# A decoder layer on one core: PE's instructions in the order in which the program writes them, sums of weight blocks one half product earlier

## The chip, the core and the metric

The kernel runs on one core of one Trainium2 chip. A core has five engines with a queue of instructions each: PE (TensorE, matmuls), DVE (VectorE), ACT (ScalarE), POOL (GpSimd) and SP (SyncE, which here only issues DMAs). They meet in semaphores: an instruction waits until those that it depends on have signalled. The metric is the time of one execution on the device, in microseconds (us), as the median of several runs.

## What is computed

One layer with three gated branches over 256 positions of width 2048 in float32, cut to what matters:

```python
q_a, k_a, v_a, z_a, u_g, v_g, z_g, q_c, z_c, g_logit = split(x @ w_in)   # 9 of width 1024, g_logit 6144
y_a = block_attention(q_a, k_a, v_a) * silu(z_a)              # 8 heads, causal
y_g = spatial_gating(u_g, v_g, w_s, ...) * silu(z_g)          # 8 groups
y_c = memory_attention(q_c, mem @ w_mem_k, mem @ w_mem_v) * silu(z_c)    # 4 heads
gates = sigmoid(g_logit)                                      # one per branch
merged = gates[0] * (y_a @ w_branch_attn) + gates[1] * (y_g @ w_branch_sgu) + gates[2] * (y_c @ w_branch_mem)
out = layer_norm(alpha * x + merged @ w_out)
```

With 256 positions there is one block of the block attention, so each head is causal attention over 256 keys.

## The kernel before

**Products.** Every large product of float32 values is made of three passes: each operand is split into a high and a low part (hi and lo), and hi x hi, hi x lo and lo x hi are added up in PSUM. `split(hi, lo, v)` is two instructions: ACT copies v to hi (L59), DVE subtracts hi from v (L60). A weight therefore passes DMA, ACT and DVE before PE can use it.

**Two streams.** The *classic* stream (a generator, `classic()`) multiplies weights half chunk by half chunk. Half chunk h17_0 is the first half of chunk 17, its parts are hi17_0 and lo17_0, 128x1024 each; there are three buffers for each part, and `c_half` prepares two halves ahead. Its parts in order: the gate of the memory branch (zc), queries (qc) and the memory attention, three tiles of za, a gated branch b2, the rest of za, queries and keys (q, k) of the block attention, three tiles of ug, branch b0, the rest of ug, zg with the spatial gating, branch b1. A *channel tile* (`channel_tile`, L187 and L188) is two halves of 8 k-steps, each with one 512-column and one 256-column matmul; a half of a branch (L712 to L714) is 12 matmuls of 512 columns.

The *S stream* (`s_stream`) makes the other projections with a fast matrix product: 8 units of 7 products (M1, M5, M6, M3, M7, M4, M2), each in two halves, 112 *half products* s0 to s111 of 12 matmuls (L386 to L388). Its weights are four blocks of a unit, B11, B12, B22 and B21 (in the listings b0 to b3), 128x2048 for each half. Before M5, M6 and M4 the block B11 is replaced by a difference (another block less B11) on DVE (L311); that is what "sum of weight blocks" means here. The block that a half product needs is then split into sh and sl (`s_prep`). These share a tag, shl, with four buffers, which is two half products: the split for half product s+2 can begin only when PE is done with half product s.

**Stages before the streams.** First the memory's values (mv) and keys (mk0 to mk7, channel tiles), then the two streams in turn. The driver takes 160 classic steps and, in proportion, 112 S steps, with a lead of 2 and a tail of 14 classic steps.

**Heads.** Each attention head has three small steps on PE: scores, transposes of the softmax's p (mpt0 to mpt3 for the memory heads, pt0 to pt7 for the others) and values. They are put in `pending`, and `tick` emits one step at the end of each classic tile. Between scores and transposes stand the maximum (DVE), two exponentials (ACT), a reciprocal and two scales (DVE, L587 for a block head: `p<-p,sm`).

**Order.** The lists `late` and `pending` set the order in which the program writes its instructions (the order of emission). The order in which an engine issues them is not that: for every engine a scheduler, which goes by a simulated timeline, chooses among the instructions whose operands it thinks ready. So on PE matmuls of the two streams are mixed finely, and a head's transposes come when the scheduler finds a place.

The names that the steps below touch: `s_prep` (splits and sums for a half product), `s_stream` (calls `s_prep(s + 2)` after half product s), `joined` (evacuates a channel tile: ACT copies one half of PSUM, named mk5l, zc0l and so on, DVE adds the other), `mem_head` and `moba_head` (the heads).

Of the kernel before, what the change touches and what calls it, by code (L numbers as in the profile page):

```python
# [11 lines left out]
ALU = mybir.AluOpType  # L12
# [15 lines left out]
def decoder_layer(ctx, tc, xT, memT, x_tok, w_st, w_mv, w_mk, w_zc, w_qc, w_za, w_qk, w_ug, w_zg,  # L28
                  w_br, w_o, w_sT, sgu_bc, ln_g, ln_b, out):
    nc = tc.nc  # L30

    const = ctx.enter_context(tc.tile_pool(name="const", bufs=1))
    big = ctx.enter_context(tc.tile_pool(name="big", bufs=1))
# [17 lines left out]
    def new_sps(name):  # L51
        return psum.tile([P, 512], F32, tag="sps", name=name, bufs=3)
# [5 lines left out]
    def split(hi, lo, v):  # L58
        nc.scalar.activation(hi, v, AF.Copy)  # L59
        nc.vector.tensor_tensor(lo, v, hi.bitcast(F32), op=ALU.subtract)  # L60
# [224 lines left out]
    UNITS = 8  # L285
    PRODUCTS = ("M1", "M5", "M6", "M3", "M7", "M4", "M2")
    FORM = {"M5": 1, "M6": 2, "M3": 4, "M7": 3}
    rt, shl, xsf, sp = {}, {}, {}, {}

    def s_load(u, blk, h):  # L290
        if u >= UNITS:
            return
        tag, bufs = ("rA", 2) if blk == 0 else ("rB", 4)
        t = wts.tile([P, 2048], F32, tag=tag, name=f"b{blk}_{u}_{h}", bufs=bufs)
        nc.sync.dma_start(t, w_st[u, blk, h])
        rt[u, blk, h] = t

    B11, B12, B22, B21 = range(4)

    def s_prep(s):  # L300
        u, r = divmod(s, 14)
        if u >= UNITS:
            return
        p, h = divmod(r, 2)
        p = PRODUCTS[p]
        if p in FORM:
            t = wts.tile([P, 4, 2 * P], F32R, tag="xsf", name=f"xf{s}", bufs=3)
            nc.sync.dma_start(t.bitcast(F32), xf_d[FORM[p], h])
            xsf[s] = t
        b = lambda blk: rt[u, blk, h]  # L310
        sub = lambda o, x, y: nc.vector.tensor_tensor(o, x, y, op=ALU.subtract)  # L311
        src = {"M1": B11, "M5": B11, "M6": B11, "M4": B11, "M3": B22, "M7": B12, "M2": B21}[p]
        if p == "M5":
            sub(b(B11), b(B12), b(B11))
        elif p == "M6":
            sub(b(B11), b(B22), b(B11))
        elif p == "M4":
            sub(b(B11), b(B21), b(B11))
        hi = wts.tile([P, 2048], F32R, tag="shl", name=f"sh{s}", bufs=4)
        lo = wts.tile([P, 2048], F32R, tag="shl", name=f"sl{s}", bufs=4)  # L320
        split(hi, lo, b(src))
        shl[s] = (hi, lo)
        if p == "M3":
            sub(b(B12), b(B22), b(B12))
            s_load(u, B21, h)
        elif p == "M7":
            s_load(u + 1, B12, h)
        elif p == "M4":
            s_load(u + 1, B11, h)
        elif p == "M2":  # L330
            s_load(u + 1, B22, h)

    def snap(name):
        return work.tile([P, 512], F32, tag="snap", name=name, bufs=5)

    def s_stream(finish):

        bank, kept = {}, {}

        def keep(name, ps):  # L340
            kept[name] = snap(name)
            nc.scalar.activation(kept[name], ps, AF.Copy)

        def result(u, t, n, ps, name):
            r = kept[name]
            nc.vector.tensor_tensor(r, ps, r, op=ALU.add)
            finish(u, t, n, r)

        def evacuate(u, p):
            if p == "M1":  # L350
                keep(f"k1_{u}", bank["b"])
            elif p == "M5":
                keep(f"k5_{u}", bank["d"])
            elif p == "M6":
                keep(f"k6_{u}", bank["b"])
            elif p == "M3":
                result(u, 0, 1, bank["d"], f"k6_{u}")
            elif p == "M7":
                keep(f"k7_{u}", bank["b"])
                result(u, 1, 1, bank["b"], f"k5_{u}")  # L360
            elif p == "M4":
                result(u, 1, 0, bank["c"], f"k7_{u}")
            else:
                result(u, 0, 0, bank["a"], f"k1_{u}")

        BANK = {"M1": "b", "M6": "b", "M7": "b", "M5": "d", "M3": "d", "M4": "c", "M2": "a"}
        for s in range(14 * UNITS):
            u, r = divmod(s, 14)
            p, h = divmod(r, 2)
            p = PRODUCTS[p]  # L370
            if h == 0 and p in ("M1", "M5", "M4", "M2"):
                bank[BANK[p]] = new_sps(f"s{p}_{u}")
            ps = bank[BANK[p]]
            hi, lo = shl.pop(s)
            for kk in range(4):
                k = 4 * h + kk
                if p in FORM:
                    ah, al = xsf[s][:, kk, 0:P], xsf[s][:, kk, P:2 * P]
                else:
                    k += 0 if p == "M1" else 8  # L380
                    t = P if p == "M4" else 0
                    ah, al = xhl[:, k, t:t + P], xhl[:, k, S + t:S + t + P]
                c = slice(kk * 512, (kk + 1) * 512)
                first = h == 0 and kk == 0 and p in ("M1", "M5", "M4", "M2")
                last = h == 1 and kk == 3
                nc.tensor.matmul(ps, ah, hi[:, c], start=first, stop=False, skip_group_check=True)  # L386
                nc.tensor.matmul(ps, ah, lo[:, c], start=False, stop=False, skip_group_check=True)  # L387
                nc.tensor.matmul(ps, al, hi[:, c], start=False, stop=last, skip_group_check=True)  # L388
            xsf.pop(s, None)
            s_prep(s + 2)  # L390
            if h == 1:
                late.append(lambda u=u, p=p: evacuate(u, p))
            yield
# [76 lines left out]
    while x_work:  # L470
        x_work.pop(0)()
        step(lambda: None)
    s_prep(0)
    s_prep(1)


    yhl = {}
# [297 lines left out]
    C_STEPS, S_STEPS = 160, 14 * UNITS  # L775
    LEAD, TAIL = 2, 14
    cs, ss = classic(), s_stream(s_finish)
    done_c = done_s = 0
    for _ in run(cs):
# [136 lines left out]
```

## Time and profile before

| | us |
|---|---|
| median of 3 runs | 1010.97 (1009.83 to 1012.68) |
| profiled execution, its own time | 1014.38 |
| its span | 1012.7 |
| PE busy | 982.4 (97%) |
| weight loads on PE, beside matmuls | 826.9 (82%) |
| DVE busy | 820.6 (81%) |
| ACT busy | 590.6 (58%) |
| POOL busy | 12.0 (1%) |
| mean granted TensorE clock | 0.99 |

The profiled execution lies above the median, so the numbers of a trace are set against its own time. A share of busy time is a mean over stages. PE's idle time stands where an instruction waits at the head of its queue, and the list of waits says for whom. Matmuls overlap: one of 512 columns is shown 0.39 us long, and the next starts 0.23 us after it. The granted clock of a stretch is 1.0 at 2.4 GHz and 0.5 at 1.2 GHz.

### The profile page before, as it was taken

How to read it: one execution, taken by the hardware profiler on the slowest of the kernel's cores; microseconds unless marked ns; L12 is line 12 of the kernel's file. 1: busy time of each engine (PE TensorE's matmuls, PEld its weight loads, DVE VectorE, ACT ScalarE, POOL GpSimd, SP SyncE). 2: the span in 40 equal slices, each digit the busy share in tenths (PEclk: the TensorE clock that was granted, in tenths of full speed). 3: DMA queues.
4: the chain of work that ended last, by engine and by line, in shares of the span. 5: the costliest groups of instructions: out<-in, count | busy, mean ns of one | idle time of the engine just before them, and what ended most of it. 6: DMA issues, size and time to landing. Idle time of an engine off the chain costs nothing.

```text
span 1012.7 us, 12913 instructions
## 1 busy us (share of the span) xinstructions
PE 982.4 (97%) x4888; PEld 826.9 (82%) x4888; DVE 820.6 (81%) x800; ACT 590.6 (58%) x646; POOL 12.0 (1%) x17
## 2 busy tenths in 40 slices
PE   9999899999999999999999999979998999999995
PEld 7788788888888788888888888858877888878885
DVE  5865987898779799888979898899979877676657
ACT  5654665565577566556556566867555559554430
POOL 0000000000000000000000000000000010000000
PEclk9999999999999999999999999989999999999998
DMA  8899589738965897598379648937994785778622
GB/s 330 313 387 414 181 304 348 277 132 296 364 223 168 295 382 278 165 362 346 134 271 356 236 139 281 382 106 269 414 366 147 284 286 183 249 259 303 238 84 83
DMA packets 68126, 269.28 MB, mean 266 GB/s; under 512 B 7521, under 2 KB 21601, under 8 KB 45537
## 3 DMA queue, kind: packets, MB, share of 16 engines
q1 hardware_dynamic: 68064, 268.47, 72.2%
q8 instruction: 38, 0.62, 0.2%
q14 instruction: 24, 0.19, 0.0%
HBM read 245.37 MB, written 23.07 MB: 265 GB/s over the span
## 4 chain that ended last, share of the span: by engine, by line
PE 85%; DVE 5%; ACT 4%; DMA 3%; issue 2%; POOL 0%; SPq 0%; DVEq 0%; ACTq 0%
PE sM L386 9%; PE sM L387 9%; PE sM L388 9%; PE b L713 4%; PE b L714 3%; PE b L712 3%; PE zc L187 3%; PE k L187 3%; PE qc L187 3%; PE za L187 3%; PE q L187 3%; PE mk L187 3%; PE o L800 3%; PE o L799 3%; PE o L798 3%; PE mv L423 3%
## 5 line engine op out<-in xcount | busy, mean ns | idle before, releaser
L59 ACT ACTIVATE hi<-raw 128x1024 fp32r<-128x1024 f32 (+1 forms) x218 | 228.3, 1051 | 191.4 <-PE o L800 29.1
L60 DVE TENSOR_TENSOR lo<-raw,hi 128x1024 fp32r<-128x1024 f32 (+1 forms) x218 | 263.1, 1214 | 77.2 <-ACT hi L59 76.4
L60 DVE TENSOR_TENSOR sl<-b,sh 128x2048 fp32r<-128x2048 f32 x112 | 256.3, 2291 | 57.1 <-ACT sh L59 56.7
L59 ACT ACTIVATE sh<-b 128x2048 fp32r<-128x2048 f32 x112 | 214.4, 1915 | 99.6 <-PE sM L387 89.3
L311 DVE TENSOR_TENSOR b<-b,b 128x2048 f32<-128x2048 f32 x64 | 146.3, 2289 | 8.0 <-DMA b<-in_w_st_dram 7.8
L386 PE MATMUL sM<-sh,xf 128*128 128x512 f32 x256 | 101.3, 396 | 6.5 <-ACT sh L59 6.5
L387 PE MATMUL sM<-sl,xf 128*128 128x512 f32 x256 | 100.6, 393 | 2.5 <-DVE sl L60 2.5
L388 PE MATMUL sM<-sh,xf 128*128 128x512 f32 x256 | 100.2, 391 | 0.0
L387 PE MATMUL sM<-sl,xhl 128*128 128x512 f32 x192 | 76.8, 400 | 0.6 <-DVE sl L60 0.6
L386 PE MATMUL sM<-sh,xhl 128*128 128x512 f32 x192 | 77.4, 403 | 0.0
L713 PE MATMUL b<-lo,yhl 128*128 128x512 f32 x192 | 76.1, 397 | 1.2 <-DVE lo L60 1.2
L388 PE MATMUL sM<-sh,xhl 128*128 128x512 f32 x192 | 76.3, 397 | 0.0
L714 PE MATMUL b<-hi,yhl 128*128 128x512 f32 x192 | 74.9, 394 | 0.0
L712 PE MATMUL b<-hi,yhl 128*128 128x512 f32 x192 | 74.0, 398 | 0.9 <-ACT hi L59 0.9
L386 PEld LDWEIGHTS sM<-sh,xf 128*128 128x128 f32 x256 | 48.3, 189 | 18.3 <-ACT sh L59 7.9
L387 PEld LDWEIGHTS sM<-sl,xf 128*128 128x128 f32 x256 | 48.2, 188 | 12.9 <-DVE sl L60 3.2
L388 PEld LDWEIGHTS sM<-sh,xf 128*128 128x128 f32 x256 | 48.1, 188 | 10.3
L187 PE MATMUL ug<-xhl,hi 128*128 128x512 f32 x128 | 46.3, 400 | 1.5 <-ACT hi L59 1.5
L187 PE MATMUL q<-xhl,hi 128*128 128x512 f32 x128 | 46.5, 399 | 0.0
L187 PE MATMUL qc<-xhl,hi 128*128 128x512 f32 x128 | 46.2, 400 | 0.0
L187 PE MATMUL zc<-xhl,hi 128*128 128x512 f32 x128 | 45.7, 398 | 0.4 <-ACT hi L59 0.4
L187 PE MATMUL k<-xhl,hi 128*128 128x512 f32 x128 | 46.0, 397 | 0.0
(296 smaller groups left out, 1853.1 us busy)
## 6 DMA issues: line engine op xcount, KB each, us to landing
b<-in_w_st_dram SPq DMA_DIRECT2D x64, 1024.0 KB, 7.2
xf<-xf SPq DMA_DIRECT2D x64, 512.0 KB, 6.0
raw<-in_w_br_dram SPq DMA_DIRECT2D x24, 1024.0 KB, 6.8
raw<-in_w_qk_dram SPq DMA_DIRECT2D x16, 1024.0 KB, 7.3
raw<-in_w_o_dram SPq DMA_DIRECT2D x16, 1024.0 KB, 5.4
raw<-in_w_mk_dram SPq DMA_DIRECT2D x8, 1024.0 KB, 10.1
raw<-in_w_zc_dram SPq DMA_DIRECT2D x8, 1024.0 KB, 6.5
raw<-in_w_qc_dram SPq DMA_DIRECT2D x8, 1024.0 KB, 7.6
```

The source lines that it names most:

```text
L59: nc.scalar.activation(hi, v, AF.Copy)
L60: nc.vector.tensor_tensor(lo, v, hi.bitcast(F32), op=ALU.subtract)
L187: nc.tensor.matmul(ps, hi, x, start=first, stop=False)
L311: sub = lambda o, x, y: nc.vector.tensor_tensor(o, x, y, op=ALU.subtract)
L386: nc.tensor.matmul(ps, ah, hi[:, c], start=first, stop=False, skip_group_check=True)
L387: nc.tensor.matmul(ps, ah, lo[:, c], start=False, stop=False, skip_group_check=True)
L388: nc.tensor.matmul(ps, al, hi[:, c], start=False, stop=last, skip_group_check=True)
L423: nc.tensor.matmul(ps[t][n], lhs, rhs[:, n * 512:(n + 1) * 512], start=(k == 0 and rhs is hi and lhs is xh[t]), stop=(k == KT - 1 and lhs ...
L712: nc.tensor.matmul(ps[t], yh, hi[:, c], start=(k == 0), stop=False)
L713: nc.tensor.matmul(ps[t], yh, lo[:, c], start=False, stop=False)
L714: nc.tensor.matmul(ps[t], yl, hi[:, c], start=False, stop=(k == 7))
L798: nc.tensor.matmul(ps[:, 0:n], mh, hi, start=first, stop=False)
```

## The change

PE is taken from the scheduler: its instructions stand in the order of emission. The other four engines are still ordered by the scheduler. And the subtraction that turns B11 into the block for M5, M6 or M4 leaves `s_prep` for a function of its own, `s_sum`, which is called for half product s+3 after half product s, ahead of `s_prep(s + 2)`, and for half product 2 ahead of the streams. The other subtraction, of B12 in M3's preparation, stays.

```diff
--- before.py
+++ after.py
@@ -28,6 +28,7 @@
 def decoder_layer(ctx, tc, xT, memT, x_tok, w_st, w_mv, w_mk, w_zc, w_qc, w_za, w_qk, w_ug, w_zg,
                   w_br, w_o, w_sT, sgu_bc, ln_g, ln_b, out):
     nc = tc.nc
+    ctx.enter_context(tc.manual_schedule(engines={mybir.EngineType.PE}))
 
     const = ctx.enter_context(tc.tile_pool(name="const", bufs=1))
     big = ctx.enter_context(tc.tile_pool(name="big", bufs=1))
@@ -297,6 +298,17 @@
 
     B11, B12, B22, B21 = range(4)
 
+    def s_sum(s):
+
+        u, r = divmod(s, 14)
+        if u >= UNITS:
+            return
+        p, h = divmod(r, 2)
+        other = {"M5": B12, "M6": B22, "M4": B21}.get(PRODUCTS[p])
+        if other is not None:
+            o = rt[u, B11, h]
+            nc.vector.tensor_tensor(o, rt[u, other, h], o, op=ALU.subtract)
+
     def s_prep(s):
         u, r = divmod(s, 14)
         if u >= UNITS:
@@ -310,12 +322,6 @@
         b = lambda blk: rt[u, blk, h]
         sub = lambda o, x, y: nc.vector.tensor_tensor(o, x, y, op=ALU.subtract)
         src = {"M1": B11, "M5": B11, "M6": B11, "M4": B11, "M3": B22, "M7": B12, "M2": B21}[p]
-        if p == "M5":
-            sub(b(B11), b(B12), b(B11))
-        elif p == "M6":
-            sub(b(B11), b(B22), b(B11))
-        elif p == "M4":
-            sub(b(B11), b(B21), b(B11))
         hi = wts.tile([P, 2048], F32R, tag="shl", name=f"sh{s}", bufs=4)
         lo = wts.tile([P, 2048], F32R, tag="shl", name=f"sl{s}", bufs=4)
         split(hi, lo, b(src))
@@ -387,6 +393,7 @@
                 nc.tensor.matmul(ps, ah, lo[:, c], start=False, stop=False, skip_group_check=True)
                 nc.tensor.matmul(ps, al, hi[:, c], start=False, stop=last, skip_group_check=True)
             xsf.pop(s, None)
+            s_sum(s + 3)
             s_prep(s + 2)
             if h == 1:
                 late.append(lambda u=u, p=p: evacuate(u, p))
@@ -472,6 +479,7 @@
         step(lambda: None)
     s_prep(0)
     s_prep(1)
+    s_sum(2)
 
 
     yhl = {}
```

All engines issue the same instructions as before, but for the loads of ACT's function table, of which there are 34 in place of 30. Three places show what moves. In the listings a row is a line of the program, the operation, output and inputs; a number at the end of a name is a buffer's.

PE around the transposes of head 1 of the block attention (pt1; q4 and q3 are the channel tiles of two later heads' queries), before:

```order
L188 MATMUL q4_4352<-xhl_96,lo56_0_4277 128x256
L187 MATMUL q4_4352<-xhl_96,hi56_0_4276 128x512
L597 MATMUL pt1_4155<-ident_83,p1_4074 128x128
L188 MATMUL q4_4352<-xhl_96,lo56_0_4277 128x256
L597 MATMUL pt1_4155<-ident_83,p1_4074 128x128 x2
L187 MATMUL q4_4352<-xhl_96,hi56_0_4276 128x512
```

and after, where the last matmuls of half product s57 stand ahead (sM1_4 is its PSUM tile):

```order
L392 MATMUL sM1_4_4094<-sh57_4017,xhl_98 128x512
L393 MATMUL sM1_4_4094<-sl57_4018,xhl_98 128x512
L394 MATMUL sM1_4_4094<-sh57_4017,xhl_98 128x512
L605 MATMUL pt1_4158<-ident_85,p1_4077 128x128 x3
L188 MATMUL q3_4166<-xhl_98,hi54_0_4045 128x512
L189 MATMUL q3_4166<-xhl_98,lo54_0_4046 128x256
```

In the order of emission all three transposes stand between s57 and the first half of q3; before, they stood within q4, two tiles later.

DVE at the same head (p1 is its softmax, sm1 its sum; sl58 to sl60 are low parts of S half products, lo55 and lo56 of classic halves, kT2 and qT3 other heads' evacuations), before:

```order
L60 TENSOR_TENSOR sl59_4149<-b0_4_1_3795,sh59_4148 128x2048
L311 TENSOR_TENSOR b0_4_0_3753<-b2_4_0_3843,b0_4_0_3753 128x2048
L60 TENSOR_TENSOR lo55_1_4207<-raw55_4022,hi55_1_4206 128x1024
L585 RECIPROCAL sm1_4077<-sm1_4077 128x2
L60 TENSOR_TENSOR lo56_0_4277<-raw56_4115,hi56_0_4276 128x1024
L208 TENSOR_TENSOR qT3_4161<-q3_4163,q3l_4247 128x256
L311 TENSOR_TENSOR b0_4_1_3795<-b2_4_1_3927,b0_4_1_3795 128x2048
L587 TENSOR_SCALAR p1_4074<-p1_4074,sm1_4077 128x128
L587 TENSOR_SCALAR p1_4074<-p1_4074,sm1_4077 128x256
L60 TENSOR_TENSOR sl60_4203<-b0_4_0_3753,sh60_4202 128x2048
```

and after:

```order
L61 TENSOR_TENSOR sl59_4152<-b0_4_1_3797,sh59_4151 128x2048
L310 TENSOR_TENSOR b0_4_0_3756<-b2_4_0_3845,b0_4_0_3756 128x2048
L593 RECIPROCAL sm1_4080<-sm1_4080 128x2
L310 TENSOR_TENSOR b0_4_1_3797<-b2_4_1_3929,b0_4_1_3797 128x2048
L595 TENSOR_SCALAR p1_4077<-p1_4077,sm1_4080 128x128
L595 TENSOR_SCALAR p1_4077<-p1_4077,sm1_4080 128x256
L61 TENSOR_TENSOR lo55_1_4210<-raw55_4025,hi55_1_4209 128x1024
L61 TENSOR_TENSOR sl60_4206<-b0_4_0_3756,sh60_4205 128x2048
```

The scales of p1 now stand two classic low parts and an evacuation earlier, and still behind sl59 and two sums.

DVE at the start of the two streams (unit 0's blocks b0, b1, b2; chunk 17 is the second zc tile), before:

```order
L60 TENSOR_TENSOR lo16_1_891<-raw16_723,hi16_1_890 128x1024
L60 TENSOR_TENSOR sl0_918<-b0_0_0_775,sh0_917 128x2048
L208 TENSOR_TENSOR mk7_913<-mk7_864,mk7l_914 128x256
L311 TENSOR_TENSOR b0_0_0_775<-b1_0_0_551,b0_0_0_775 128x2048
L208 TENSOR_TENSOR zc0_1058<-zc0_993,zc0l_1059 128x256
L311 TENSOR_TENSOR b1_0_0_551<-b2_0_0_777,b1_0_0_551 128x2048
L60 TENSOR_TENSOR sl1_922<-b0_0_1_833,sh1_921 128x2048
L60 TENSOR_TENSOR sl2_1080<-b0_0_0_775,sh2_1079 128x2048
L311 TENSOR_TENSOR b0_0_1_833<-b1_0_1_608,b0_0_1_833 128x2048
L311 TENSOR_TENSOR b0_0_0_775<-b2_0_0_777,b0_0_0_775 128x2048
L60 TENSOR_TENSOR lo17_0_995<-raw17_841,hi17_0_994 128x1024
L60 TENSOR_TENSOR lo17_1_1016<-raw17_841,hi17_1_1015 128x1024
```

and after:

```order
L61 TENSOR_TENSOR sl0_920<-b0_0_0_777,sh0_919 128x2048
L61 TENSOR_TENSOR lo16_1_893<-raw16_725,hi16_1_892 128x1024
L310 TENSOR_TENSOR b0_0_0_777<-b1_0_0_553,b0_0_0_777 128x2048
L209 TENSOR_TENSOR mk7_915<-mk7_866,mk7l_916 128x256
L323 TENSOR_TENSOR b1_0_0_553<-b2_0_0_779,b1_0_0_553 128x2048
L61 TENSOR_TENSOR sl1_924<-b0_0_1_835,sh1_923 128x2048
L209 TENSOR_TENSOR zc0_1061<-zc0_996,zc0l_1062 128x256
L310 TENSOR_TENSOR b0_0_1_835<-b1_0_1_610,b0_0_1_835 128x2048
L323 TENSOR_TENSOR b1_0_1_610<-b2_0_1_837,b1_0_1_610 128x2048
L61 TENSOR_TENSOR lo17_0_998<-raw17_843,hi17_0_997 128x1024
L61 TENSOR_TENSOR lo17_1_1019<-raw17_843,hi17_1_1018 128x1024
```

The sums of both halves now stand ahead of lo17_0, sl2 behind it. On PE the order there is zc0's second half, h17_0 (zc1), s0, h17_1, s1; before it was zc0's second half, s0, one matmul of s1, one of s2, the rest of s1 and of s2, and then h17_0.

ACT in the keys stage, where hi14_0 is the half that PE multiplies right behind tile mk5, before:

```order
L207 ACTIVATE mk4l_769<-mk4_692 128x256
L59 ACTIVATE hi14_0_748<-raw14_614 128x1024
L59 ACTIVATE hi14_1_779<-raw14_614 128x1024
L207 ACTIVATE mk5l_826<-mk5_747 128x256
L59 ACTIVATE hi15_0_805<-raw15_670 128x1024
```

and after:

```order
L208 ACTIVATE mk4l_771<-mk4_694 128x256
L208 ACTIVATE mk5l_828<-mk5_749 128x256
L60 ACTIVATE hi14_0_750<-raw14_616 128x1024
L60 ACTIVATE hi14_1_781<-raw14_616 128x1024
L60 ACTIVATE hi15_0_807<-raw15_672 128x1024
```

The evacuation mk5l moved ahead of both halves of chunk 14.

## Rows read from the trace of the kernel before

**Rows 1.** The page: busy us (share of the span), number of instructions.

```profile
PE 982.4 (97%) x4888; PEld 826.9 (82%) x4888; DVE 820.6 (81%) x800; ACT 590.6 (58%) x646; POOL 12.0 (1%) x17
```

**Rows 2.** PE's list of waits: total us, number, longest.

```profile
PE sM L386 <- ACT sh L59: 6.5, 3, 2.8
...
PE mix L668 <- POOL ws L657: 1.8, 1, 1.8
```

**Rows 3.** Table of windows: length, engines' busy us (instructions), granted clock, DMA.

```profile
100.00:150.00 50.00, 46.71 (x232) 38.86 (x231) 44.83 (x31) 29.88 (x31) 0.00 (x0) 0.97 0.68 240
650.00:700.00 50.00, 44.80 (x176) 35.16 (x175) 45.17 (x42) 37.54 (x40) 0.00 (x0) 0.90 0.55 203
700.00:750.00 50.00, 48.47 (x222) 40.04 (x221) 43.48 (x40) 28.64 (x25) 0.00 (x0) 1.00 0.99 391
750.00:800.00 50.00, 45.70 (x235) 38.03 (x234) 46.06 (x40) 27.32 (x28) 3.45 (x1) 1.00 0.55 193
```

**Rows 4.** Timeline of PE, 667 to 773: start, length, matmul, [idle before, releaser].

```profile
667.71 0.50 PE L386 MATMUL sM<-sh,xf 128*128 128x512 f32 x1 [2.38 <-ACT sh L59]
...
668.83 0.63 PE L387 MATMUL sM<-sl,xhl 128*128 128x512 f32 x1
...
772.50 0.50 PE L387 MATMUL sM<-sl,xf 128*128 128x512 f32 x1 [1.83 <-DVE sl L60]
```

**Rows 5.** Timeline of ACT, the keys stage.

```profile
86.87 0.39 ACT L207 ACTIVATE mk5l<-mk 128x256 f32<-128x256 f32 x1 [0.88 <-PE mk L188]
```

**Rows 6.** Timeline of PE, start of the S stream.

```profile
103.31 0.39 PE L386 MATMUL sM<-sh,xhl 128*128 128x512 f32 x1
...
109.28 0.80 PE L386 MATMUL sM<-sh,xf 128*128 128x512 f32 x1 [2.84 <-ACT sh L59]
...
111.16 0.63 PE L387 MATMUL sM<-sl,xhl 128*128 128x512 f32 x1
111.58 0.63 PE L388 MATMUL sM<-sh,xhl 128*128 128x512 f32 x1
```

**Rows 7.** Timeline of DVE, same place.

```profile
97.97 2.29 DVE L60 TENSOR_TENSOR sl<-b,sh 128x2048 fp32r<-128x2048 f32 x1 [0.58 <-ACT sh L59]
```

**Rows 8.** Timeline of PE, half product s17.

```profile
219.13 0.40 PE L386 MATMUL sM<-sh,xf 128*128 128x512 f32 x1
```

**Rows 9.** Timeline of DVE, head 0 of the memory attention.

```profile
224.77 1.22 DVE L60 TENSOR_TENSOR lo<-raw,hi 128x1024 fp32r<-128x1024 f32 x1
225.90 0.62 DVE L527 TENSOR_SCALAR mp<-mp,msm 128x256 f32<-128x256 f32 x2
```

**Rows 10.** Timeline of PE, around head 1 of the block attention.

```profile
493.46 0.39 PE L187 MATMUL q<-xhl,hi 128*128 128x512 f32 x1
...
512.46 0.27 PE L597 MATMUL pt<-ident,p 128*128 128x128 f32 x1
```

**Rows 11.** Timeline of ACT, same place.

```profile
493.44 1.92 ACT L59 ACTIVATE sh<-b 128x2048 fp32r<-128x2048 f32 x1 [1.29 <-PE sM L387]
```

**Rows 12.** Timeline of DVE, same place.

```profile
497.03 2.29 DVE L60 TENSOR_TENSOR sl<-b,sh 128x2048 fp32r<-128x2048 f32 x1
499.23 2.29 DVE L311 TENSOR_TENSOR b<-b,b 128x2048 f32<-128x2048 f32 x1
...
502.56 0.17 DVE L585 RECIPROCAL sm<-sm 128x2 f32<-128x2 f32 x1
...
504.09 2.29 DVE L311 TENSOR_TENSOR b<-b,b 128x2048 f32<-128x2048 f32 x1
506.29 0.55 DVE L587 TENSOR_SCALAR p<-p,sm 128x128 f32<-128x128 f32 x2
```

**Rows 13.** The page's groups: operation, count, busy us, mean ns, idle before, releaser.

```profile
L59 ACT ACTIVATE hi<-raw 128x1024 fp32r<-128x1024 f32 (+1 forms) x218 | 228.3, 1051 | 191.4 <-PE o L800 29.1
L60 DVE TENSOR_TENSOR lo<-raw,hi 128x1024 fp32r<-128x1024 f32 (+1 forms) x218 | 263.1, 1214 | 77.2 <-ACT hi L59 76.4
...
L59 ACT ACTIVATE sh<-b 128x2048 fp32r<-128x2048 f32 x112 | 214.4, 1915 | 99.6 <-PE sM L387 89.3
```

## The prediction

> **What bounds the kernel now.** I read the busy lines first. PE is busy 982.4 us of 1012.7, so at most 30.3 us are idle [rows 1], and nothing in the change removes a matmul. Next the table of windows: it says where those 30 us lie and where the clock was low. Four windows matter. Between 650 and 800 us PE is idle for 5.2, 1.5 and 4.3 us, 11.0 in all, and the granted clock of 0.90 in the first of them costs another 5.0 (0.10 of 50); between 100 and 150 us it is idle for 3.3 [rows 3]. Most of the rest lies in the start and the tail, which the change hardly reaches. The list of waits names the releasers: S matmuls waiting for a split on ACT lead with 6.5 us, and a single wait for POOL is 1.8 [rows 2]. The long gaps, read one by one, are all of a kind: the scheduler let PE start a half product whose split was late, while ready halves of the other stream stood behind it [rows 4]. So the matmuls' own length sets the end, and a new order can win back about 16 us (11.0 and 5.0) at most, 18 if the drain around each gap counts. Whatever it adds in waits is added to the end, since PE is never the idle engine elsewhere.
>
> The Trainium skill ("Perfetto Trace Analysis", section "Identifying the Most-Contended Engine") calls matmul busy time a poor measure and asks for the busy share of the weight loads. By that, 82% [rows 1] would leave 18%, or an estimated 186 us, to win. The trace disagrees for this purpose: 512-column matmuls start 0.23 us apart with no gap at full clock, whatever the loads do, and a change of order alters no spacing.
>
> **What the change does to the orders.** Only PE is taken from the scheduler. ACT, DVE, POOL and SP are still ordered by it, and the order listings show that it does not put the operations that PE now waits for first. That matters because an in-order PE that meets a late operand waits with everything behind it, in both streams. Moving the sums of weight blocks costs no time of its own: there are as many as before, on the same engine. It only changes what stands ahead of what on DVE. Four more loads of ACT's function table fall to an engine that is busy 58% [rows 1] and are hidden; where they stand ahead of a split that PE waits for, the bounds below take them in. On SP the loads of raw19 and raw20 no longer stand behind one that waits for s2: earlier, and nobody waits for them. POOL's order is the same. I take the places in order of time. For each, the excess is against the profiled run.
>
> *Keys stage, +3.* ACT now makes mk5l, the evacuation of tile mk5, before hi14_0, the split of the half that PE multiplies right after mk5. Before, mk5l came behind both halves and began at 86.87, when PE ended that tile [rows 5]. So PE now waits there for mk5l (0.39), a split (1.05 on ACT) and its low part on DVE (1.2) [rows 13], 2.6 us; with some tenths for the first stage, whose matmuls meet the low parts two earlier, I take 3. Ends 0, if PE reaches that half later for other reasons, and 4.
>
> *Start of the S stream, +5.* Before, PE went from zc0 to half products s0 (at 103.31), s1 and s2, idled 2.84 us for one split between them and then ran seven matmuls 0.43 us apart, half clock (1.2 GHz), before 0.23 returned [rows 6]. That is 2.8 and about 1.5 lost. Now zc1's half h17_0 stands behind zc0. Its low part lo17_0 stands on DVE behind sl0, lo16_1, a sum, mk7, a subtraction, sl1, zc0, a sum and a subtraction. With sl0 at 97.97 [rows 7] and 2.2 us for each of the six large ones, 1.13 for lo16_1 and 0.34 for each of the two small ones, lo17_0 starts at 97.97 + 13.2 + 1.13 + 0.68 = 113.0 and ends at 114.1. PE has zc0 done near 104.2, 0.9 later than before (lo16_1 is done only at 97.97 + 2.2 + 1.13 = 101.3, and a half takes 2.75), and idles nearly 10 us. By 117.1 the old order had done s0, s1 and s2, 8.25 us of work past zc0 (103.31 + 8.25 + the 4.3 lost + some tenths); the new one has done about 3.0. The difference is 5.3, less what old stalls return after it; I take 5, between 2 (the sums placed ahead find their data early) and 7 (a half-clock stretch of 1.5 on top).
>
> *First memory head, +5.* The transposes mpt0 now stand right behind s17. In the old order a classic half came in between, after the first matmul of s17 at 219.13 [rows 8], and mpt0 stood only behind s18. In emission order s17 begins at the same point and ends at 219.13 + 12 x 0.23 = 221.9. The two scales of mp0 ran from 225.90 to 226.5, right behind a lo of 1.13, with no idle time of DVE [rows 9]; that lo now stands behind them, so they are done at 225.4. The wait is 3.5; with a half-clock stretch of 1.5 after a wait of that length (as after 2.84 [rows 6] and 2.38, where matmuls of 0.63 follow, but not after 1.83 [rows 3, 4]) 5. Ends 0, if DVE is earlier there by as much as PE was late before, and 6.
>
> *Head 1 of the block attention, +12.3.* This is the largest term. The transposes pt1 now stand between s57 and q3's first half. PE passed that point at 493.46; in the old order pt1 came at 512.46, in the midst of q4 [rows 10]. On DVE the two scales of p1 stand behind sl59, a sum, a reciprocal and a second sum. sl59 needs sh59, which reuses the buffers of s57 and so starts on ACT when s57 ends: 493.44, released by PE [rows 11]. From there the old rows give sl59 at 497.03, a sum at 499.23, so RECIPROCAL at 501.43, the second sum at 501.5 and the scales from 503.7 to 504.2, 2.6 earlier than the 506.29 of before, since two lo and qT3 now stand behind [rows 12]. PE waits from 493.46 to 504.2, 10.8, and 1.5 for the clock after. Behind the transposes wait q3's halves and s58, whose splits are ready, and behind those ACT's next splits, for whose buffers s58 must end; so nothing is done meanwhile that would be late otherwise. The low end: with DVE free, 1.92 (sh59) + 2.2 (sl59) + 2.2 + 0.1 + 2.2 + 0.46 = 9.1. It can't be less, since the chain starts from the very block that PE finishes. High end 13.
>
> *Heads 3 and 6, +6 each.* The same knot, shorter: p3's scales stand behind sl65, whose buffers are those of s63, directly ahead of pt3; p6's behind sl75 and s73. The wait is 1.92 (sh) + 2.2 (sl) + 0.46 (scales) = 4.6 [rows 11 to 13], and 1.5 for the clock. Together 12, between 9 (no clock loss) and 15. The page's 89.3 us of ACT's splits waiting for PE [rows 13] shows how tight those buffers are all along.
>
> *Small places, +2.* Heads 2 and 5, accumulators of a gated branch that are evacuated a step later, and the output stage: each some tenths to 1 us, 0 to 6 in all.
>
> *What goes, -14.* The stalls between 650 and 800 us: the 16 above [rows 3], since in strict turn no half product is started ahead of its split, less about 2 for the mix that still waits for POOL [rows 2]. Ends -18 and -8: in that stretch DVE is busy 45.17 of 50 [rows 3], so an unlucky turn can keep half the loss.
>
> The sum: 3 + 5 + 5 + 12.3 + 12 + 2 - 14 = +25.3. The profiled execution took 1014.4 (span 1012.7 and 1.7 around it), so it becomes 1039.7; that run was 3.4 above the median of 1011.0, so I forecast 1036.3, rounded to **1036**. All low ends give +2, all high ends about +43 (1013 to 1054).
>
> **Rivals.** *Faster, 1002.* The stalls go in full (-18), the S start costs no more than before, and the heads' other waits are covered, because DVE, no longer late, has softmax steps done within the 8.3 us (two classic halves and one half product of 2.75 each) that PE has between scores and transposes. Then only the 9.1 of head 1 remains: 1014.4 - 18 + 9.1 - 3.4 = 1002. It decides at whether sh65 and sh75 start before s63 and s73 end; four shl buffers hold just two half products, which speaks against it. *No change, about 1013.* All waits at their low ends, no clock loss: +2, by which the gain in the b0 and ug stages pays for the heads. For it: after 1.83 us of idle the clock did not fall [rows 3, 4]. Against: the waits worked out are longer than that. *Much slower, about 1056.* The knot of heads 3 and 6 is met by heads 0, 2, 4, 5 and 7 as well, some 4 us at each, because a delayed DVE never regains its lead (about 20 more than forecast). For it: DVE is busy nine tenths in these stretches, and each wait for the buffers recurs. Against: while PE waits, DVE empties its queue, and in the listing these heads' scales don't stand behind a split that needs the block just ahead. *That the change does nothing* is excluded by the order listing, in which PE's rows are the emission's.
>
> **How the numbers follow.** Forecast 0.72, faster 0.08, no change 0.06, much slower 0.14. A measurement of this kernel can't tell 0.3%, some 3 us, from nothing. Faster by more than that: the faster rival and a sliver of the others, 0.09; within it 0.05; slower 0.86. The range of 8 in 10 runs from 1017, where most terms stand at their low ends, to 1056, where the forecast's high ends and half of the much slower case lie.
>
> **What would show it.** Right: PE's waits are led by transposes on DVE's scales (pt1 some 10 us, pt3 and pt6 near 5, mpt0 near 4), a gap of near 10 us around 104 to 114 us on a low part, PE without gaps past 1 us in the b0 and ug stages, and a granted clock of 0.5 just behind the long waits. Wrong: pt1's wait under 5 us, which would mean that DVE's order on the chip doesn't decide; waits for sh and sl of the S stream that remain between 650 and 800 us; or waits at all eight heads.

## The result and the profile after

The changed kernel takes 1050.2 us (median of 4 runs, 1046.5 to 1052.1), the kernel before 1010.6 beside it: a ratio of 1.038, 95% interval 1.035 to 1.042, slower. The forecast was 1036 in a range of 1017 to 1056: the right way, 14 us too low. The execution whose trace is read here took 1048.37 us, 34.0 more than the one of before (1014.38).

The page of the changed kernel, its busy line:

```profile
PE 988.0 (94%) x4888; PEld 831.0 (79%) x4888; DVE 821.2 (78%) x800; ACT 596.2 (57%) x650; POOL 19.0 (2%) x17
```

PE's busy time rose by 5.6 us only, against [rows 1]; DVE's and ACT's shares fell. The time went into PE's idle time and into stretches at the lower clock. PE's list of waits names it (total us, number, longest):

```profile
PE pt L605 <- DVE p L595: 21.7, 4, 10.7
PE zc L188 <- ACT hi L60: 4.4, 1, 4.4
PE zc L189 <- DVE lo L61: 3.5, 1, 3.5
PE b L720 <- DVE sg L734: 3.4, 2, 2.7
PE mpt L542 <- DVE mp L535: 3.3, 1, 3.3
...
PE mk L188 <- ACT hi L60: 1.8, 2, 1.4
...
PE sM L393 <- DVE sl L61: 1.1, 1, 1.1
```

Before, the S matmuls' wait for a split on ACT led with 6.5 us, and POOL's was 1.8 [rows 2]. Both are gone; one 1.1 us wait for a split of the S stream is left. In their place stand the heads' transposes (L605 and L542) waiting for DVE's scales, and the start of the S stream (zc). The table of windows (length, busy us of PE, PEld, DVE, ACT and POOL, granted clock, DMA) shows where:

```profile
50.00:100.00 50.00, 46.71 (x249) 39.71 (x248) 25.87 (x30) 20.58 (x27) 0.00 (x0) 0.97 1.00 397
500.00:550.00 50.00, 39.26 (x192) 33.04 (x191) 36.78 (x38) 22.00 (x29) 0.00 (x0) 0.86 0.30 104
550.00:600.00 50.00, 45.61 (x230) 38.58 (x229) 35.23 (x40) 26.07 (x33) 0.00 (x0) 0.97 0.85 305
600.00:650.00 50.00, 43.48 (x217) 36.51 (x216) 43.54 (x42) 25.64 (x32) 0.00 (x0) 0.93 0.43 148
650.00:700.00 50.00, 48.87 (x239) 40.85 (x239) 35.92 (x35) 40.45 (x47) 0.00 (x0) 1.00 0.82 310
700.00:750.00 50.00, 47.31 (x202) 38.64 (x202) 48.99 (x44) 34.78 (x33) 0.00 (x0) 0.97 0.65 239
750.00:800.00 50.00, 50.00 (x250) 42.12 (x249) 47.06 (x49) 29.83 (x28) 0.00 (x0) 1.00 1.01 376
```

Between 650 and 800 us PE is now idle for 3.8 us where it was 11.0, and the clock is 1.00, 0.97 and 1.00 [rows 3]: that is the gain. Between 500 and 650 us it is idle for 21.7.

Such windows mix idle time and clock. So for the accounts below each pair of neighbouring matmuls in a trace was compared with the usual distance of their starts (0.23 us for 512 columns, 0.12 for 256, 0.11 for 128, but 0.22 for the 256-column matmuls of the heads), and what was above it added up. This *lost time* is 43.9 us in the trace of before and 77.2 in that of after; the difference, 33.3, is nearly the 34.0 of the two executions. A row is one execution: that of *both* is 2.6 us faster than its median, that of *both, PE in order from step 8* 3.1 us slower, the others of the changed programs lie within 2. By stretch of the trace:

| kernel | 0 to 150 us | 150 to 450 | 450 to 650 | 650 to 800 | rest | all |
|---|---|---|---|---|---|---|
| before | 12.7 | 4.5 | 4.6 | 18.9 | 3.2 | 43.9 |
| the change | 25.1 | 8.3 | 32.5 | 7.2 | 4.1 | 77.2 |
| transposes a tick later | 25.4 | 4.2 | 10.4 | 5.3 | 3.9 | 49.2 |
| sums kept back | 19.7 | 10.6 | 18.6 | 11.7 | 3.9 | 64.5 |
| both | 19.3 | 6.0 | 4.2 | 6.3 | 3.6 | 39.4 |
| both, PE in order from step 8 | 14.4 | 8.0 | 4.1 | 9.8 | 3.9 | 40.2 |
| the same, sums kept back later | 12.0 | 6.0 | 4.1 | 6.8 | 4.7 | 33.6 |
| the change from step 96 on | 12.6 | 4.0 | 16.2 | 7.3 | 3.6 | 43.7 |

The largest wait, at head 1 of the block attention, on PE (start, length, operation, idle time before it and who ended it):

```profile
510.07 0.39 PE L394 MATMUL sM<-sh,xhl 128*128 128x512 f32 x1
521.20 0.87 PE L605 MATMUL pt<-ident,p 128*128 128x128 f32 x3 [10.74 <-DVE p L595]
521.72 0.78 PE L188 MATMUL q<-xhl,hi 128*128 128x512 f32 x1
...
522.51 0.63 PE L188 MATMUL q<-xhl,hi 128*128 128x512 f32 x1
```

and on DVE in the same place:

```profile
514.11 2.28 DVE L61 TENSOR_TENSOR sl<-b,sh 128x2048 fp32r<-128x2048 f32 x1
516.31 2.28 DVE L310 TENSOR_TENSOR b<-b,b 128x2048 f32<-128x2048 f32 x1
...
518.59 2.27 DVE L310 TENSOR_TENSOR b<-b,b 128x2048 f32<-128x2048 f32 x1
520.78 0.54 DVE L595 TENSOR_SCALAR p<-p,sm 128x128 f32<-128x128 f32 x2
```

The order is the one that the listing gave: split, sum, reciprocal, sum, scales. PE's half product ended at 510.3, the transposes came at 521.20; the rows of before that answer are [rows 10, 12]. Behind the wait the 512-column matmul and its 256-column partner take 0.79 us together (521.72 to 522.51 by their starts) in place of 0.35, and the pairs that follow 0.64.

### The profile page after: what moved, and what is told of

Same layout as the page of the kernel before. It is cut to its first block, busy times and chain, and to the rows that moved or that the text cites. A ratio compares the mean times of both kernels' runs of the same rounds, so it can differ in the third digit from the quotient of the medians.

```text
span 1046.6 us, 12926 instructions
## 1 busy us (share of the span) xinstructions
PE 988.0 (94%) x4888; PEld 831.0 (79%) x4888; DVE 821.2 (78%) x800; ACT 596.2 (57%) x650; POOL 19.0 (2%) x17
## 4 chain that ended last, share of the span: by engine, by line
PE 80%; DVE 10%; DMA 4%; ACT 3%; issue 3%; SPq 0%; DVEq 0%; ACTq 0%
PE sM L392 8%; PE sM L394 8%; PE sM L393 8%; PE b L720 3%; PE b L721 3%; PE b L722 3%; PE q L188 3%; PE o L807 3%; PE zg L188 3%; PE qc L188 3%; PE o L806 3%; PE o L808 3%; PE zc L188 3%; PE k L188 3%; PE ug L188 3%
## 5 line engine op out<-in xcount | busy, mean ns | idle before, releaser
L310 DVE TENSOR_TENSOR b<-b,b 128x2048 f32<-128x2048 f32 x48 | 109.6, 2283 | 1.3 <-DMA b<-in_w_st_dram 1.2
L720 PE MATMUL b<-hi,yhl 128*128 128x512 f32 x192 | 76.1, 396 | 3.4 <-DVE sg L734 3.4
L722 PE MATMUL b<-hi,yhl 128*128 128x512 f32 x192 | 75.4, 393 | 0.0
L392 PEld LDWEIGHTS sM<-sh,xf 128*128 128x128 f32 x256 | 48.0, 188 | 10.8
L188 PE MATMUL zc<-xhl,hi 128*128 128x512 f32 x128 | 47.9, 413 | 4.4 <-ACT hi L60 4.4
L188 PE MATMUL q<-xhl,hi 128*128 128x512 f32 x128 | 49.7, 425 | 0.0
L188 PE MATMUL mk<-memhl,hi 128*128 128x512 f32 x128 | 46.5, 405 | 1.8 <-ACT hi L60 1.8
```

The lines of the kernel that those rows point to most:

```text
L188: nc.tensor.matmul(ps, hi, x, start=first, stop=False)
L310: nc.vector.tensor_tensor(o, rt[u, other, h], o, op=ALU.subtract)
L720: nc.tensor.matmul(ps[t], yh, hi[:, c], start=(k == 0), stop=False)
L722: nc.tensor.matmul(ps[t], yl, hi[:, c], start=False, stop=(k == 7))
```

## The experiments

All are built from the changed kernel. Each is given with the kernel before run beside it on the same chip; its median there was 1011.6 to 1012.2.

**One half of the change does nothing by itself.** The order listings tell this without a run. A kernel in which only PE's order is changed prints the same rows on all five engines as the changed kernel, and one in which only the sums move prints the same as the kernel before. It fits that the scheduler takes a sum when its block is free, wherever the program writes it. So all that follows is PE's order, and the other engines' answer to it.

**Transposes one tick later.**

```diff
-        return fetch, [scores, transposes, values]
+        return fetch, [scores, lambda: None, transposes, values]
...
-        return [scores, transposes, values]
+        return [scores, lambda: None, transposes, values]
```

> PE in the order of emission as in the change, but each head's transposes are emitted one tick later (an empty step between scores and transposes). Theory A: the four waits for the scales of p (21.7 us) and the one for mp (3.3) in the changed kernel come from where the transposes stand on PE, behind a half product whose end starts the chain that DVE does ahead of the scales. With a tick more, the chain of head 1 (split 1.9 and 2.2, sum 2.2, a low part 1.1, an evacuation 0.3, scales 0.5, some 8.3 us) starts behind s58, and two classic halves and s59 (8.3 us) cover it. Those 25 us go, and about 6 us of half clock behind them: about 1020 us, 1015 to 1026. Rival B: PE in strict turn makes DVE the bound in these stretches, and the wait only moves to the next split: under 10 us gained, 1040 to 1048, with new waits for sh and sl.

1019.2 us, 1.007 times the kernel before (1.006 to 1.009), so 31 us less than the change. PE's waits:

```profile
PE zc L188 <- ACT hi L60: 4.4, 1, 4.4
PE pt L605 <- DVE p L595: 4.2, 1, 4.2
PE zc L189 <- DVE lo L61: 3.8, 1, 3.8
```

Of 25 us at the heads 4.2 are left, all at head 1: its scales stand behind a split, a sum, a low part and qT3, the evacuation of another tile. The waits at the start are untouched. Theory A holds, with its number, but for the 4.2 us at head 1.

**Other engines in the order of emission, too.**

```diff
-    ctx.enter_context(tc.manual_schedule(engines={mybir.EngineType.PE}))
+    ctx.enter_context(tc.manual_schedule(engines={mybir.EngineType.PE, mybir.EngineType.DVE}))
```

and the same with Activation in place of DVE, or with both.

> PE and DVE both in the order of emission; ACT, POOL and SP as the scheduler puts them. In the emission the scales of a head stand directly behind its scores, ahead of the splits that are emitted later. Theory A (it is DVE's order that makes PE wait): the waits at pt1, pt3 and pt6 (20.5 us) fall under 3 us in all, and the start of the S stream loses its 3.5 us wait for lo17_0. DVE itself now waits for ACT's exponentials at 12 heads, some 2 us each, which PE's lead of two halves should cover: 1015 to 1030 us. Rival B (the lead of two halves is too small for any order): waits for sl and lo rise by what the waits for p fall, 1040 to 1060.

> PE and ACT both in the order of emission; DVE, POOL and SP as the scheduler puts them. Theory A: the loss in the keys stage (two waits of 2.6 us in all at 89 us, 1.5 at 62 us and a half clock stretch of 1.7) and the 4.4 us wait for hi17_0 come from ACT's order, in which an evacuation or a SiLU that waits stands ahead of the split that PE needs next. In the emission the splits stand ahead: those 6 us and 4.4 us go, the waits for p (21.7) stay, since they stand on DVE: 1036 to 1044. Rival B: the splits are late because their weights land late, so ACT's order changes under 2 us there: 1046 to 1052.

> PE, DVE and ACT in the order of emission, POOL and SP as the scheduler puts them. Theory A: each engine's order now agrees with PE's, so both groups of waits go, and so do the stalls that the kernel before had between 650 and 800 us: 985 to 1010 us, faster than the kernel before. Rival B: an order in which evacuations and softmax steps stand where they are written makes ACT and DVE wait at the head of their queues for PE (a split of s+2 is emitted directly behind half product s and waits for its end, with the next classic split behind it), so PE runs dry at each turn: over 1040 us.

With DVE in order: 1110.9 us (ratio 1.097, 1.095 to 1.100). With ACT: 1048.6 (1.037, 1.035 to 1.040). With both: 1097.5 (1.085, 1.084 to 1.087). PE's waits with DVE in order:

```profile
PE b L720 <- DVE sg L734: 37.1, 9, 6.0
...
PE pt L605 <- DVE p L595: 6.9, 2, 4.1
```

The wait at pt fell, but from 21.7 to 6.9, not under 3, and a wait that I had not reckoned with is worth 37.1: a gated branch (b) needs two of three accumulators for each column block, and their evacuation `gated` is written one step late. DVE's timeline at the longest of them:

```profile
345.33 2.29 DVE L61 TENSOR_TENSOR sl<-b,sh 128x2048 fp32r<-128x2048 f32 x1
347.53 1.22 DVE L61 TENSOR_TENSOR lo<-raw,hi 128x1024 fp32r<-128x1024 f32 x1
348.67 2.29 DVE L61 TENSOR_TENSOR sl<-b,sh 128x2048 fp32r<-128x2048 f32 x1
350.87 1.29 DVE L734 TENSOR_TENSOR sg<-b,sg 128x512 f32<-128x512 f32 x2
```

PE ended the accumulator's last matmul at about 345.5 and stood until 351.61 for L734, which reads it, while DVE did two S splits and a classic one that stand ahead of it in the program. So both theories miss: DVE's order does decide, but the order of emission is no better a one. It puts other late work ahead of what PE needs. With both in order the same accumulators lead:

```profile
PE b L720 <- DVE sg L734: 40.4, 9, 8.1
```

The number there is rival B's (over 1040), but its reason, PE running dry behind S splits that wait at the head of their queues, is not what the list shows: the waits for those splits come to 2.6 us. With ACT in order the number is rival B's too, and theory A was right on the keys stage alone:

```profile
PE b L721 <- DVE lo L61: 9.7, 6, 2.6
PE zc L188 <- ACT hi L60: 7.5, 2, 4.4
PE pt L605 <- DVE p L595: 3.6, 3, 1.4
```

The waits in the keys stage (mk) are gone but for 0.2 us, but 3.1 us appear at the next tile, zc0, and the 4.4 us for hi17_0 stay: ACT does that split now behind sh1, which waits 6.56 us for its block's DMA, so rival B's reason holds for this one.

```profile
111.55 1.91 ACT L60 ACTIVATE sh<-b 128x2048 fp32r<-128x2048 f32 x1 [6.56 <-DMA b<-in_w_st_dram]
113.36 1.99 ACT L60 ACTIVATE hi<-raw 128x1024 fp32r<-128x1024 f32 x2
```

The waits for p, which I had expected to stay, fell to 3.6, because DVE's scheduler made another order. In their place come fourteen waits of 0.8 to 2.9 us for high and low parts, past 150 us. The lost time is that of the changed kernel, 77.2 us.

**Sums kept back.** The sums on DVE may not move ahead of what the program writes before them.

```diff
-            nc.vector.tensor_tensor(o, rt[u, other, h], o, op=ALU.subtract)
+            tc.keep_in_program_order(nc.vector.tensor_tensor(o, rt[u, other, h], o, op=ALU.subtract))
...
-        sub = lambda o, x, y: nc.vector.tensor_tensor(o, x, y, op=ALU.subtract)
+        sub = lambda o, x, y: tc.keep_in_program_order(nc.vector.tensor_tensor(o, x, y, op=ALU.subtract))
```

> The changed kernel with one thing more: the sums of weight blocks, both kinds, may not move ahead of DVE instructions that the program writes before them. In its listing p1's scales now stand ahead of sl59, with one sum ahead of them; p6's stand ahead of sl75; p3's still stand behind sl65; lo17_0 has two sums ahead, not four. Theory A (the length of a wait is set by what stands between the end of the half product and the scales): pt1 falls from 10.7 to about 3 us, pt6 from 5.3 to under 1, pt3 stays at 4 to 5.5, the second wait at the start of the S stream from 3.5 to under 2, and 3 to 6 us of half clock go: 1028 to 1036 us. Rival B (the total work of DVE there sets the wait, not its order): the sum of the waits at pt stays over 17 us: 1044 to 1052.

1035.9 us, 1.024 (1.022 to 1.026). The wait at head 1 on PE's timeline is now:

```profile
509.51 0.61 PE L605 MATMUL pt<-ident,p 128*128 128x128 f32 x3 [2.53 <-DVE p L595]
```

Head 1 waits 2.53 in place of 10.74: sl59 and one sum now stand behind its scales. This is the plainest test of the chain, since PE's order there is the same and so is DVE's amount of work. Head 3, whose scales still stand behind a split, waits 6.5, 1.0 more than expected; head 6 waits 0.9, as expected, but head 7, which did not wait before, waits 2.5. In all 12.5 us are left at pt, so rival B (over 17) is out, and the time lies at theory A's upper end. At the start of the S stream the second wait fell from 3.5 to 1.3 and the first from 4.4 to 3.1.

**Both, and a seam.** The second kernel below also leaves PE to the scheduler until classic step 8:

```diff
-    ctx.enter_context(tc.manual_schedule(engines={mybir.EngineType.PE}))
...
         done_c += 1
+        if done_c == 8:
+            ctx.enter_context(tc.manual_schedule(engines={mybir.EngineType.PE}))
```

> Transposes one tick later as in the first run, and the sums kept back. Theory A: the 4.2 us that were left at pt1 go (p1's scales stand ahead of one sum and sl59), with some 3 us of half clock, and 1 to 2 us of the wait for lo17_0: 1009 to 1015. Rival B: kept back, the sums make the S splits late, with new waits for sh and sl: 1019 or more.

> As the run before, but PE keeps the scheduler's order until classic step 8, past the keys stage and the start of the two streams; the order of emission holds from there on. Theory A: the first 150 us cost what they cost before the change (12.7 us above the matmuls' own spacing, where the first run had 25.4), the later stages what the first run had without pt1's wait (some 17): 993 to 1002 us, faster than the kernel before. Rival B: the kernel before needs its order of the first 150 us and its later run-ahead together, and a lead that is lost at the seam comes back as waits: 1005 or more.

Both edits without a seam: 1012.7, 1.001 (1.000 to 1.003), no difference from the kernel before. With the seam: 1008.2, 0.996 (0.995 to 0.997). In the first no wait for p is left (the table's 4.2 us between 450 and 650 is the level of before), as theory A has it. The second is faster, but by less than A said, and its number is B's: past 150 us its trace loses 25.8 us, where A reckoned with 17, with 6.0 us of waits for accumulators and one of 2.4 for a low part of the S stream; 3.1 of the difference belong to that execution, which is so much slower than the median. In the first 150 us it lost 14.4, not 12.7.

**The part with the forecast gain alone.** The same seam in the changed kernel at step 96, the end of the block attention.

> The changed kernel, but PE keeps the scheduler's order until classic step 96, the end of the block attention; the order of emission holds for ug, the branch b0, zg and b1 alone. It is the part of the change for which a gain was forecast, by itself. Theory A: the stalls between 650 and 800 us go as in the changed kernel, where this stretch cost 7.2 us above the matmuls' spacing and 18.9 before, less a wait for the scales of head 6 or 7 of up to 5: 998 to 1006 us. Rival B: that stretch was short of stalls in the changed kernel only because PE, held up earlier, had left ACT and DVE time to get ahead; alone it gains under 3 us: 1008 to 1013.

1013.4, 1.001 (1.000 to 1.002): no gain. The time is B's (0.4 above its range), the reason isn't:

```profile
PE pt L604 <- DVE p L594: 7.1, 2, 4.5
```

The stretch from 650 to 800 us lost 7.3 us, as in the whole change, against 18.9 before, so the stalls there go without any earlier waits. But past the seam the transposes of heads 5 and 6 still wait on DVE (4.54 and 2.60, with a half-clock stretch behind each), 11.6 us more than before between 450 and 650. What the order of emission gains in b0 and ug, two heads give back.

**A better version.** The seam at step 8, transposes a tick later, and the sums kept back only from half product 8 on, or not at all:

```diff
-            nc.vector.tensor_tensor(o, rt[u, other, h], o, op=ALU.subtract)
+            ins = nc.vector.tensor_tensor(o, rt[u, other, h], o, op=ALU.subtract)
+            if s >= 8:
+                tc.keep_in_program_order(ins)
...
```

The other subtraction is held in the same way.

> Transposes one tick later; PE in the scheduler's order until classic step 8 and in the order of emission from there on; sums kept back only from half product 8 on, so that the first unit's sums move ahead as they did before the change. Theory A: the first 150 us cost 12.7 us above the matmuls' spacing as in the kernel before (the run with everything kept back had 14.4 there, the one without a seam 19.3), the rest about 20 as in the run without a seam: 33 in place of the 43.9 of before, 1000 to 1005 us. Rival B: what an order in the first 150 us wins or loses is taken up by slack later, so the time stays at that of the run before, 1007 to 1010.

> The same without keeping any sum back. Theory A: past 150 us it costs what the first run cost there, 24 us, most of the difference to the run before this one being the wait at pt1 (4.2) and its half clock: 1004 to 1009 us, 3 to 5 slower than that one. Rival B: with PE's earlier lead, DVE's order comes out another way and no wait at pt1 is left: within 2 us of the run before this one.

1005.3 us, 0.994 (0.992 to 0.995), and 1006.3, 0.994 (0.993 to 0.995). Both beat the kernel before and, by 44 us, the changed one. In the first, 33.6 us are lost, 12.0 of them in the first 150 us, as theory A had it. PE's longest entry is now the accumulators of the branches:

```profile
PE b L725 <- DVE sg L739: 5.1, 4, 2.0
```

In the second the wait at pt1 is back (4.2 us) and 36.1 us are lost in all, so that the two differ by 1 us, not 3 to 5: the sums' place is worth little once the transposes stand later.

**The sums' earlier place, where it can act.** In the first of these two the sums are kept where they are written, so the second half of the change has an effect there. Undone:

```diff
+        s_sum(s)
         hi = wts.tile([P, 2048], F32R, tag="shl", name=f"sh{s}", bufs=4)
...
-            s_sum(s + 3)
             s_prep(s + 2)
...
-    s_sum(2)
```

> As the run with the seam at step 8 and the sums kept back from half product 8 on, but a sum is written directly ahead of its split, as before the change, not one half product earlier. It tells what the second part of the change is worth where it can act at all (with sums that float freely, DVE's order is the same with and without it). Theory A: written at the split, the sum of 2.2 us lengthens the chain from the end of half product s to the split of s+2 (sum 2.2, sh 1.9, sl 2.2, 6.3 us against a classic half of 2.75 and a half product of 2.75), so S splits come late in units' M5, M6 and M4, and it is 5 to 15 us slower: 1010 to 1020. Rival B: the block is free long before, and DVE makes the sum in time either way: within 2 us of 1005.

1006.1, 0.995 (0.993 to 0.996): within 1 us, as rival B has it. One half product more of lead for the sums buys nothing that can be measured.

## Why the prediction held, and where it was off

The lost time by place, after less before, beside the terms of the sum:

| place | forecast | trace |
|---|---|---|
| first stage and keys | +3 | +6.7 |
| start of the S stream | +5 | +5.7 |
| memory head 0 | +5 | +3.3 |
| block head 1 | +12.3 | +13.2 |
| block head 3 | +6 | +6.0 |
| block head 6 | +6 | +7.4 |
| small places | +2 | +2.8 |
| stalls between 650 and 800 us | -14 | -11.7 |
| sum | +25.3 | +33.3 |

For the waits at the heads the mechanism is the one forecast: PE in strict turn waits where DVE's order, still the scheduler's, puts an operation late. The waits themselves came out close: 10.7 us at head 1 for 10.8, 4.4 at head 3 and 5.3 at head 6 for 4.6, 3.3 at memory head 0 for 3.5. That these waits belong to the place of the transposes and not to a short DVE is shown by the first run, and that what stands ahead of the scales sets their length by the run with the sums kept back.

*The keys stage was mis-sized.* The wait that mk5l causes is there, 1.42 for hi14_0 and 0.75 for its low part:

```profile
90.74 0.50 PE L188 MATMUL mk<-memhl,hi 128*128 128x512 f32 x1 [1.42 <-ACT hi L60]
92.00 0.39 PE L189 MATMUL mk<-memhl,lo 128*128 128x256 f32 x1 [0.75 <-DVE lo L61]
...
93.28 0.60 PE L188 MATMUL mk<-memhl,hi 128*128 128x512 f32 x1
93.68 0.41 PE L189 MATMUL mk<-memhl,lo 128*128 128x256 f32 x1
```

But the term had no clock loss, and from 93.28 on the matmuls start at half-clock distances (0.40 us here, then 0.43 and 0.21); the window's granted clock of 0.97 makes that 1.5 us (0.03 of 50). And a second place, at 62 us, which I had not looked for in the listing, costs 1.5 (0.35 for a split on ACT, 0.76 for a low part, and the drains). What stands ahead of the split there is no evacuation: ACT's order has moved the split hi9_1 behind two of the S stream's input, which wait 4.40 and 0.58 us for their DMA.

*The start of the S stream* came out right in size, in part by luck, and half wrong in its cause. I had let DVE's order set one wait of near 10 us, with no clock loss. The "some tenths" of its sum, up to 117.1, are 1.2 us, in which the old order had issued two more matmuls, so its 5.3 should be 5.7. The trace has two waits, 7.9 us together, and 2.4 lost to the half clock behind them:

```profile
114.68 0.80 PE L188 MATMUL zc<-xhl,hi 128*128 128x512 f32 x1 [4.42 <-ACT hi L60]
...
118.94 0.58 PE L189 MATMUL zc<-xhl,lo 128*128 128x256 f32 x1 [3.47 <-DVE lo L61]
```

The first, 4.42 us, ends with hi17_0 on ACT, which stands there behind zc0's evacuation and its SiLU; the SiLU waits for DVE:

```profile
110.29 0.38 ACT L208 ACTIVATE zc0l<-zc 128x256 f32<-128x256 f32 x1 [3.35 <-PE zc L189]
...
113.26 0.42 ACT L499 ACTIVATE zc<-zc 128x256 f32<-128x256 f32 x1 [1.29 <-DVE zc L209]
113.59 2.93 ACT L60 ACTIVATE hi<-raw 128x1024 fp32r<-128x1024 f32 x3
```

The second, 3.47, is lo17_0, as forecast. The four sums that stand ahead of it do so without the change's second half: the listing with PE's order alone has them in the same place. So the step that let the moved sums change what stands ahead of what on DVE is wrong as put; PE's order did that.

*Memory head 0* waited 3.3 us, as worked out, but no half clock followed. The half clock that I put behind every wait of that length came behind a wait of 2.7 us in b0 and behind 1.4 and 0.75 us in the keys stage, and not behind this one. *Head 6* waited 0.7 longer than reckoned: on ACT an evacuation stands ahead of its split, which so begins 0.5 after s73's end, and DVE, still busy with an evacuation, took up the low part 0.3 after the split was done:

```profile
640.37 0.60 ACT L348 ACTIVATE k<-sM 128x512 f32<-128x512 f32 x1 [0.65 <-PE sM L394]
640.86 1.90 ACT L60 ACTIVATE sh<-b 128x2048 fp32r<-128x2048 f32 x1
```

The clock behind it cost 1.9 us, where I had put 1.5. The window's granted clock of 0.93 would give 3.5 (0.07 of 50), but the clock fell during the wait, so 2.9 us at half clock lie where PE did nothing (a row of the table of windows):

```profile
642.80:645.66 2.86, 0.00 (x1) 0.03 (x1) 2.86 (x5) 0.00 (x0) 0.00 (x0) 0.51 0.03 11
```

*The gain* was 2.3 us less. The wait for POOL that I had left in is gone; in its place PE waits 2.69 us for an accumulator of b0, at 718 us, with a half clock behind:

```profile
721.04 0.56 PE L720 MATMUL b<-hi,yhl 128*128 128x512 f32 x1 [2.69 <-DVE sg L734]
721.40 0.63 PE L721 MATMUL b<-lo,yhl 128*128 128x512 f32 x1
721.83 0.63 PE L722 MATMUL b<-hi,yhl 128*128 128x512 f32 x1
```

DVE had begun a split of 2.28 us just before the accumulator was done. I had this kind of wait among the small places, at some tenths; the sign that PE would have no gaps past 1 us in these stages did not come.

*The step from trace to median.* The traced execution came out at 1048.4 for a forecast of 1039.7, 8.7 more. From the latter I took 3.4, the old execution's distance from its median, but the new execution lies 1.8 below its own. These three make the 13.9 between 1036.3 and 1050.2.

Of the rivals, faster and no change are out: the chain behind s57 was as long as its rows said. Much slower, 1056, is near in time, but not in its mechanism: heads 0, 2, 4 and 7 of the block attention don't wait, and head 5 waits 1.2. What was said of the weight loads' share is borne out: it is 79% in a kernel that takes 34 us longer and 82% before, and the best order found here won 7 us, so it told nothing of what an order can win or lose.

What stays open is why the clock falls behind one wait and not behind another of the same length, and why with a seam at step 8 the sums kept back from the start cost some 3 us more than when they are kept back from half product 8 on (1008.2 and 1005.3; the traces differ by 6.6, of which 3.1 are the slower execution's); both were seen, not taken apart.

## What to carry to other kernels

Taking one engine from the scheduler fixes its order, but not that of the engines that feed it: before doing so, list for each operand of the fixed engine what stands ahead of its producer, and look first for a producer that stands behind something released by the very block ahead of the consumer. That is a wait of known length, the sum of a few rows. Writing the consumer one step later costs a line in each of two functions and here gave back 31 us; putting ACT in the program's order as well gave back nothing that can be measured, and with DVE in it 47 to 61 us more were lost, over half of them in waits for evacuations that are written late (37.1 and 40.4 us, where the changed kernel has 3.4). And when a rewrite moves code that a scheduler places, compare the listings with that part alone: here half the change printed the same rows.

## What the runs showed of the hardware

In the trace of the changed kernel the length of a single wait doesn't tell whether the clock falls to 1.2 GHz. Behind 3.31 us of idle PE at memory head 0 the matmuls kept their distance,

```profile
238.06 0.72 PE L542 MATMUL mpt<-ident,mp 128*128 128x128 f32 x4 [3.31 <-DVE mp L535]
...
238.97 0.40 PE L188 MATMUL qc<-xhl,hi 128*128 128x512 f32 x1
...
239.32 0.39 PE L188 MATMUL qc<-xhl,hi 128*128 128x512 f32 x1
```

0.35 us from one 512-column matmul to the next with its partner (238.97 to 239.32), while behind 2.69 us at 718 they took 0.43 each without a partner, and behind 10.74 at head 1 0.79 with one, then 0.64.
